# Letting the scheduler place GpSimd's sums on VectorE, and keeping one part's finished weight operands in DRAM for the second token half

## The chip, the cores and the metric

The kernel runs on one core of a Trainium2 chip. The metric is the device time of one execution in microseconds (us). Engines are named as in the profile: PE is TensorE (matmuls; PEld its weight loads), DVE is VectorE, ACT is ScalarE, POOL is GpSimd, SP is SyncE, which here issues nearly all DMAs.

## What is computed

One encoder layer on 2048 tokens of width 1024: windowed grouped-query attention (16 query heads, 4 key/value heads, 64 wide, a window of 128 tokens to either side, a sink logit and a position bias), then a SwiGLU feed-forward net of hidden size 2816. Each sub-layer has an RMSNorm ahead of it and one behind it, and a shift, a scale and a gate made from the conditioning vector `c`.

```python
mod = (c_act @ ada_w[i] + ada_b[i])[:, None, :]
sh1, sc1, g1, sh2, sc2, g2 = jnp.split(mod, 6, axis=-1)
h = rmsnorm(x, mix_norm_pre[i]) * (1.0 + sc1) + sh1
y = windowed_gqa_sink(h, att_w_qkv[j], att_w_o[j], att_sink[j], rel_bias)
x = x + g1 * rmsnorm(y, mix_norm_post[i])
h = rmsnorm(x, ffn_norm_pre[i]) * (1.0 + sc2) + sh2
y = swiglu(h, ffn_w_in[i], ffn_w_out[i])          # (silu(a) * b) @ w_out
x = x + g2 * rmsnorm(y, ffn_norm_post[i])
```

## The kernel before

**Split operands.** Every matmul operand is kept as a high and a low part (fp32r). `split` (l. 788) makes them: ACT casts the high part, DVE (in some places POOL) subtracts it from the source for the low one. `three` (l. 782) then issues three matmuls per product: high by high, high by low, low by high.

**The feed-forward net.** Both projections use a scheme of seven products in place of eight (Strassen's, in Winograd's form) on pairs of tiles. Class `Block` (l. 1359) prepares the weights of one block: two DMAs bring the raw tiles (`wir...`; the profile writes `wiri` for the input projection and `wiro` for the output projection), DVE makes four sums (`s1` to `s4`; `s_i`, `s_o` in the profile), and seven `split`s fill seven `w` tiles (`wa_i`, `ws_i`, `wa_o`, `ws_o`), each one ACT `CAST` and one DVE subtraction. `step(i)` issues the matmuls of product i: 3 per pair of hidden tiles, so 9 for a part of three pairs. `Hidden` (l. 1405) is the input projection. Its results come in pairs of hidden tiles, 11 pairs for each token half, and `give_pair` (l. 1393) writes seven operands of each pair to DRAM (`g_d`); `differences` (l. 1148) makes four of them by sums, two on POOL and two on DVE.

**The output projection.** It runs for token half 0 (1024 tokens) and then for half 1, and each half sums over the 11 pairs in parts: `PARTS = ((2, 3, 3, 3), (3, 3, 3, 2))` pairs. In each part there are four blocks `n2` = 0 to 3 of output columns; the last two are interleaved, and while they run the operands of the next part are loaded (`interleaved`, l. 1448). A part of three pairs has 4 x 7 x 9 = 252 matmuls. The part starts at pair `sum(PARTS[hf][:p])`, so half 1 goes over pairs 0 to 2, 3 to 5, 6 to 8 and at last 9 and 10, which `give_pair` has written without differences, because the last part is done without the scheme (from l. 1657). `Outs.take` (l. 1561) copies the first part's products from PSUM with ACT (`z` tiles, 31 buffers) and adds the later ones on DVE. At the end of a half the seven sums are combined (`COMBINE`, l. 1551; four of the sums on POOL), squared on ACT (`zsq`), summed on DVE (`zacc`), summed over partitions by a matmul with ones, and turned by ACT and DVE into the factor `nrz` (`rstd_out`, l. 1599; one buffer). `finish` (l. 1611) multiplies `z` by `nrz` and adds the residual `zx` on DVE and writes `out`. For half 0 this tail runs beside the first part of half 1.

**What sets the order.** Nothing of this runs in the order of the text. A `Recorder` records every operation with its engine and a cost; `forward` (l. 330) is a list scheduler over the five engines, with a port that DVE and POOL share in its model; `schedule` repeats it and keeps the order that its own model likes best, and `emit` writes that out. So all instructions carry the line of `emit`, L693 (L748 after the change), and are told apart by their tiles. Before the change each operation has one fixed engine. On SP the order is also the scheduler's: a DMA that must wait for a buffer holds those behind it.

**Other places that the prediction names.** In attention, `pr` is a block of probabilities: DVE takes the scores and a maximum (`nm`), ACT the exponential, DVE the reciprocal of the row sum (`rs`), and POOL multiplies (`pr<-pr,rs`, 128x384 or 128x256); then PE transposes it (`ident,pr`), and `phi`, `plo` and `of` are later steps of the same chain. The norm and residual behind attention (`residual`, l. 1135) are `y<-y,no`, `y<-y,xr` and `xacc`; `yacc` is the sum of squares ahead of it; they run beside the last attention blocks and the output projection of attention (`ol`, `wo`).

Of the kernel before, what the change touches and what calls it, by code (L numbers as in the profile page):

```python
# [59 lines left out]
PARTS = ((2, 3, 3, 3), (3, 3, 3, 2))  # L60
MD = max(max(p) for p in PARTS)

# [14 lines left out]
class Op:  # L77
    __slots__ = ("i", "eng", "fn", "args", "kw", "reads", "writes", "occ", "lat", "port", "table", "tiles", "pred", "succ",
                 "start", "end", "put", "prio", "npred", "ready", "ins", "bytes",
                 "wire", "out", "wait", "extra")  # L80
# [53 lines left out]
class Recorder:  # L134
# [41 lines left out]
    def record(self, eng, fn, args, kw):  # L176
# [17 lines left out]
        self.cost(op, [x for j, x in aps if j in out], [x for j, x in aps if j not in out])  # L194
# [20 lines left out]
        return op  # L215

# [113 lines left out]
    def forward(self, ahead, spare):  # L330
# [8 lines left out]
        for o in ops:  # L339
            o.npred, o.ready, o.put, o.wait, o.extra = len(o.pred), 0.0, 0, None, []  # L340
# [3 lines left out]
        port, moved = {"dve": 0.0, "pool": 0.0}, 0  # L344
# [21 lines left out]
        def offer(o):  # L366
            ready = o.ready
            for b in o.tiles:
# [6 lines left out]
            heapq.heappush(soon[o.eng], (ready, o.prio, o.i, o))  # L375

        def drop(heap, o):
            if o in heap[0]:
                heapq.heappop(heap)
            else:  # L380
                heap.pop(next(k for k, x in enumerate(heap) if o in x))
                heapq.heapify(heap)

        def wake(t):
            for u in (t, *t.later):
                if u.parked:
                    again, u.parked = u.parked, []
                    for o in again:
                        offer(o)

# [3 lines left out]
        while n < len(ops):  # L394
            best = None
            for e in ENGINES:
# [3 lines left out]
                while sn and sn[0][0] <= t:  # L400
                    r, p, i, o = heapq.heappop(sn)
                    heapq.heappush(nw, (p, i, o, r))
                if nw:
                    item, begin, src = nw[0], t, nw
                elif sn:
                    item, begin, src = sn[0], sn[0][0], sn
                    item = (item[1], item[2], item[3], item[0])
# [4 lines left out]
                if o.port:  # L412
# [4 lines left out]
            if e == "dve" and o.port and src is now[e] and begin > clock[e] + 150:  # L417
                other = [x for x in now[e] if not x[2].port]
                if other:
                    item = min(other)  # L420
                    o, begin = item[2], clock[e]
                    ask = begin
            if ahead and e in ("act", "dve", "pool") and o.put < 4:
                wait, by = 0.0, None
                for g in (e, *({"dve": ("pool",), "pool": ("dve",)}.get(e, ()) if o.port else ())):
                    for r, p, i, y in soon[g]:
                        if g != e and not y.port:
                            continue
                        if r < begin + o.occ and max(begin - o.prio, begin + o.occ - p) > max(r - p, r + y.occ - o.prio) + 50:
                            w = r + (y.lat + HOP[e] if g != e else 1.0)  # L430
                            if w > wait:
                                wait, by = w, y if g != e else None
                if wait:
                    drop(src, o)
# [3 lines left out]
                    heapq.heappush(soon[e], (wait, o.prio, o.i, o))  # L438
                    continue
            if e == "act" and o.table and o.table != table:  # L440
                stay = [x for x in now[e] if x[2].table in (None, table)]
                near = [x for x in soon[e] if x[3].table == table and x[0] < begin + 900]
                if stay and near:
                    item = min(stay)
                    o, src = item[2], now[e]
                elif near:
                    x = min(near)
                    item, src, o, begin = (x[1], x[2], x[3], x[0]), soon[e], x[3], max(begin, x[0])
            drop(src, o)
# [12 lines left out]
            if y is not None and y.npred < 0 and max(clock[e], o.ready) <= y.start + 20:  # L462
                o.extra = [y]
                begin = max(begin, y.end + HOP[e])
            if e == "act" and o.table and o.table != table:
                table = o.table
# [11 lines left out]
            else:  # L478
                end = begin + o.lat
                if o.port:  # L480
                    port[e] = begin + o.occ
            o.npred = -1
            clock[e] = begin + o.occ + (late if e == "sp" else 0)
# [18 lines left out]
            for q in o.succ:  # L502
                q.npred -= 1
                q.ready = max(q.ready, begin if o.eng == q.eng == "pe" else end + (HOP[q.eng] if o.eng != q.eng else 30))
# [127 lines left out]
    def schedule(self, rounds):  # L632
# [8 lines left out]
        for i in range(rounds):  # L641
# [4 lines left out]
            if best is None or real < best[1]:  # L646
                best = order, real, {b: b.slot for b in self.bufs.values()}, {o: o.extra for o in order if o.extra}
# [3 lines left out]
        self.slots, self.extra = best[2:]  # L651
# [4 lines left out]
    def emit(self, nc, tc, order, outside):  # L656
# [27 lines left out]
        with tc.manual_schedule():  # L684
            for o in order:
                if o.table == "log" and table != "log":
# [21 lines left out]
def encoder_layer(ctx, tc, a):  # L708
# [27 lines left out]
    wo_d = [dram.tile([P, 2, KT, P], F32, name=f"wo_d{n}") for n in range(KT)]  # L736
    cb_d = dram.tile([P, D], F32, name="cb_d")
# [621 lines left out]
    class Block:  # L1359
# [33 lines left out]
    def give_pair(hf, j):  # L1393
# [5 lines left out]
        if hf == S // HALF - 1 and j >= HT // 2 - PARTS[-1][-1]:  # L1399
# [142 lines left out]
    def part_ops(hf, p):  # L1542
        t0 = sum(PARTS[hf][:p])
# [4 lines left out]
    class Outs(Block):  # L1548
# [5 lines left out]
        def __init__(self, ops, hf, part, n2):  # L1554
            t0 = sum(PARTS[hf][:part]) * 2
            ws_ = [a["w_out"][2 * n2 + i, :, t0:t0 + 2 * ops.m] for i in range(2)]
            super().__init__(ops, n2, f"{ops.u}_{n2}", *ws_)
# [99 lines left out]
    t0, m = 2 * sum(PARTS[-1][:-1]), 2 * PARTS[-1][-1]  # L1657
# [105 lines left out]
```

## Time and profile before

| | us |
|---|---|
| runs of the kernel | 3376.76, 2058.2, 2055.8 (median 2058.2) |
| the profiled execution | 2063.44 |
| its span on the core | 2061.7 |
| PE busy | 1998.0 (97%) |
| DVE busy | 1659.1 (80%) |
| ACT busy | 1081.5 (52%) |
| POOL busy | 735.5 (36%) |
| DMA, mean of the span | 192 GB/s |

The page's list of groups says how long one instruction of a kind takes; the table by stretches says how much of a stretch each engine was busy, how much of the clock PE was granted (1.00 is all) and how much the DMAs moved; the list of waits says for which engine and tile PE waited.

The stages by that table: up to 80 us the first norm and the start of the first projection, to about 550 us the rest of it and attention, to 750 us the last attention blocks, the output projection of attention and the norms behind it, to about 1595 us the input projection of the feed-forward net, then the output projection, half 0 to about 1808 us, half 1 to the end.

### The profile page before, as it was taken

The page shows a single profiled execution, that of the slowest core. Times are in us where ns is not written, and L with a number is a line of the kernel's source. Part 1 is how long each engine was busy: PE and PEld are TensorE (multiplying, and loading weights), DVE is VectorE, ACT ScalarE, POOL GpSimd, SP SyncE. Part 2 cuts the span into 40 slices and gives each one's busy share as a digit, 9 for nine tenths or more (in the row PEclk, how much of TensorE's full clock was granted, in tenths as well). Part 3 has the DMA queues.
Part 4 walks back from the last instruction along what each step waited for, and adds up shares of the span by engine and source line. Part 5 has one row for each costly group of instructions (what it writes and reads, how often), then busy time and mean ns, then how long its engine had stood idle before and what let it go on. Part 6 is the DMA issues. An engine that isn't in the chain of part 4 may idle for free.

```text
span 2061.7 us, 28956 instructions
## 1 busy us (share of the span) xinstructions
PE 1998.0 (97%) x9366; PEld 1662.3 (81%) x9366; DVE 1659.1 (80%) x2933; ACT 1081.5 (52%) x2122; POOL 735.5 (36%) x687
## 2 busy tenths in 40 slices
PE   6999999999998999999999999999999999979997
PEld 4888888888787778888888888888888888858886
DVE  7867877765568889887878999776666799989998
ACT  5557766777687864344333633333333744455432
POOL 3413544466978624433435322222221000220030
PEclk9999999999999999999999999999999999999999
DMA  8895765486786695444446843432333554346543
GB/s 296 300 336 198 250 206 197 169 299 214 239 279 215 227 351 170 169 156 171 155 159 228 291 147 136 140 124 91 118 112 112 165 169 164 129 131 242 174 152 108
DMA packets 201667, 396.33 MB, mean 192 GB/s; under 512 B 19195, under 2 KB 61228, under 8 KB 198444
## 3 DMA queue, kind: packets, MB, share of 16 engines
q1 hardware_dynamic: 200940, 393.97, 55.7%
q8 instruction: 74, 1.21, 0.2%
q14 instruction: 77, 0.63, 0.1%
q10 hardware_dynamic: 576, 0.52, 0.1%
HBM read 270.65 MB, written 123.76 MB: 191 GB/s over the span
## 4 chain that ended last, share of the span: by engine, by line
PE 54%; DVE 2%; issue 1%; ACT 1%; POOL 0%; DMA 0%; DVEq 0%; ACTq 0%; POOLq 0%
PE bank L693 54%; DVE z L693 1%; DVE zx L693 1%; ACT nrz L693 0%; POOL z L693 0%; DVE ntz L693 0%; DMA hb22o<-g_d_b 0%; DVE ws_o L693 0%; DVE s_o L693 0%; DVE nrz L693 0%; ACT ws_o L693 0%; ACT zsq L693 0%; POOL p_i L693 0%; DVE zacc L693 0%; ACT L687 0%
## 5 line engine op out<-in xcount | busy, mean ns | idle before, releaser
L693 PE MATMUL bank<-ht,ws_i 128*128 128x512 f32 x1584 | 373.6, 389 | 0.0
L693 PEld LDWEIGHTS bank<-ht,ws_i 128*128 128x128 f32 x1584 | 297.4, 188 | 61.7
L693 PE MATMUL bank<-hb,wa_i 128*128 128x512 f32 x1056 | 254.7, 389 | 0.0
L693 PEld LDWEIGHTS bank<-hb,wa_i 128*128 128x128 f32 x1056 | 198.3, 188 | 41.1
L693 PE MATMUL bank<-ol,wo 128*128 128x512 f32 x768 | 204.0, 397 | 2.2 <-DVE ol L693 1.1
L693 DVE CUSTOM_DVE_ANT_0 pr<-bank,bias,nsink 128x384 f32<-128x384 f32 (+1 forms) x256 | 149.3, 596 | 56.8 <-PE bank L693 55.0
L693 POOL TENSOR_SCALAR pr<-pr,rs 128x384 f32<-128x384 f32 (+1 forms) x256 | 149.7, 603 | 121.6 <-DVE rs L693 115.5
L693 ACT ACTIVATE pr<-pr,nm 128x385 f32<-128x385 f32 (+1 forms) x256 | 154.9, 606 | 71.4 <-DVE nm L693 68.4
L693 POOL TENSOR_TENSOR p_i<-p_i,u_i 128x512 f32<-128x512 f32 x44 | 70.9, 1613 | 311.0 <-ACT wa_i L693 125.9
L693 ACT CAST ws_i<-s_i 128x512 fp32r<-128x512 f32 x132 | 81.9, 620 | 183.1 <-DVE s_i L693 92.9
L693 POOL TENSOR_TENSOR z<-z,z 128x512 f32<-128x512 f32 x32 | 50.2, 1586 | 357.4 <-issue 151.7
L693 DVE TENSOR_TENSOR u_i<-bank,u_i 128x512 f32<-128x512 f32 x176 | 120.7, 688 | 62.5 <-PE bank L693 61.9
L693 PEld LDWEIGHTS bank<-ol,wo 128*128 128x128 f32 x768 | 142.8, 189 | 29.4 <-DVE ol L693 1.5
L693 DVE TENSOR_TENSOR plo<-bank,phi 128x512 fp32r<-128x512 f32 x184 | 120.9, 686 | 30.9 <-ACT phi L693 28.6
L693 PE MATMUL bank<-k,q 128*128 128x384 f32 (+1 forms) x512 | 135.5, 346 | 3.7 <-DVE nm L693 3.7
L693 PE MATMUL bank<-hi,ws 128*128 128x512 f32 x384 | 134.5, 399 | 0.0
L693 DVE TENSOR_TENSOR wa_i<-wiri,wa_i 128x512 fp32r<-128x512 f32 x132 | 114.6, 868 | 21.1 <-ACT wa_i L693 18.4
L693 PE MATMUL bank<-hb,ws_i 128*128 128x512 f32 x528 | 127.0, 389 | 0.6 <-ACT p_i L693 0.6
L693 PE MATMUL bank<-ht,wa_i 128*128 128x512 f32 x528 | 127.0, 389 | 0.0
L693 ACT CAST wa_i<-wiri 128x512 fp32r<-128x512 f32 x132 | 81.1, 620 | 74.3 <-PE bank L693 70.4
L693 DVE TENSOR_TENSOR z<-bank,z 128x512 f32<-128x512 f32 (+1 forms) x164 | 107.6, 661 | 13.3 <-PE bank L693 12.7
L693 PEld LDWEIGHTS bank<-hb,ws_i 128*128 128x128 f32 x528 | 99.1, 188 | 21.5 <-ACT p_i L693 1.0
(245 smaller groups left out, 4526.7 us busy)
## 6 DMA issues: line engine op xcount, KB each, us to landing
wiri<-w_in SPq DMA_DIRECT2D x88, 512.0 KB, 4.7
ada<-ada_w SPq DMA_DIRECT2D x40, 512.0 KB, 5.0
wiro<-w_out SPq DMA_DIRECT2D x48, 384.0 KB, 3.9
q_d<-e SPq DMA_DIRECT2D x32, 512.0 KB, 4.0
q<-q_d SPq DMA_DIRECT2D x16, 1024.0 KB, 6.5
wo<-wo_d SPq DMA_DIRECT2D x16, 1024.0 KB, 5.5
g_d_b<-p_i SPq DMA_DIRECT2D x44, 256.0 KB, 3.4
g_d_t<-p_i SPq DMA_DIRECT2D x40, 256.0 KB, 2.0
```

The source lines that it names most:

```text
L693: o.ins = getattr(engs[o.eng], o.fn)(*args, **kw)
```

## The change

1. **Order of the parts.** A table `FIRST` gives the first pair of each part. Half 0 stays as it was. Half 1 now goes over pairs 2 to 4, 5 to 7, 8 to 10, and at last 0 and 1. `give_pair` follows: pairs 0 and 1 of half 1 are written without differences, 9 and 10 with them.
2. **Kept weights.** Half 0's part 1 and half 1's part 0 are now both over pairs 2 to 4 and so have the same weights. Half 0's part 1 writes each finished `w` tile to DRAM (`wk_d`; 28 writes of 128x768 f32, 384 KB each), and half 1's part 0 loads these (28 DMAs) in place of raw weights, sums and splits. That takes out 8 `wiro` DMAs, 16 DVE sums, 28 ACT `CAST`s and 28 DVE subtractions. SP issues 1220 DMAs in place of 1172.
3. **Placement.** A POOL `tensor_tensor` or `tensor_scalar` may go on DVE. `forward` offers such an operation to both engines and takes the one that is free first; on DVE only if POOL would not end it sooner (`sooner`). DVE has 3077 recorded instructions in place of 2935, POOL 506 in place of 692, ACT 1844 in place of 1872; PE has 9352 in both. So 186 operations move: 79 of the 256 multiplications `pr<-pr,rs` (71 of 128x384, 8 of 128x256), 18 small `pr<-nsink` of 128x4, 71 sums and products of 128x512 (23 of them `u_i<-u_i,b_i`, 11 of the `y` rows, 5 `xacc`, 7 `nacc`, 3 `z`), and 18 subtractions of 128x640 to 128x1024 (`w`, `ol`, `wo`, `ws`).
4. **Turn.** New too: a POOL operation that uses the shared port in the scheduler's model waits for a DVE operation that had itself been held by that port (`turn`).

```diff
+FIRST = ((0, 2, 5, 8), (2, 5, 8, 0))
...
+    def others(self, eng, fn, args, kw, ins):
+
+        if eng == "pool" and fn in ("tensor_tensor", "tensor_scalar"):
+            yield "dve", fn, args, kw
...
+            if len(o.forms) > 1 and e != o.eng_first:
+                t = sooner(o, e, begin)
+                if t is not None:
+                    later(max(begin, t) + 100)
+                    continue
...
+            if e == "pool" and uses and not o.extra and turn is not None and clock[e] - 100 < turn.start < begin:
+                o.extra = [turn]
+                begin = max(begin, turn.end + HOP[e])
+            if e == "dve" and uses:
+                turn = o if begin > ask + 100 else None
...
+    wk_d = [{n: dram.tile([P, 2, PARTS[1][0], P], F32, name=f"wk_d{i}_{n}") for n in ("a11", "s2", "a12", "s3", "s1", "a22", "s4")}
+            for i in range(KT // 2)]
...
-        def __init__(self, ops, i, u, wa, wb):
+        def __init__(self, ops, i, u, wa, wb, keep=None, kept=None):
...
+            if kept:
+                self.w = {}
+                for n, _ in self.STEPS:
+                    self.w[n] = w = pl.tile([P, 2, m, P], F32R, tag="w", bufs=wbufs, name=f"w{n}_{u}")
+                    sp.dma_start(f(w), kept[n])
+                return
...
+                if keep:
+                    sp.dma_start(keep[n], f(w))
...
-        if hf == S // HALF - 1 and j >= HT // 2 - PARTS[-1][-1]:
+        if hf == S // HALF - 1 and 0 <= j - FIRST[-1][-1] < PARTS[-1][-1]:
...
-        t0 = sum(PARTS[hf][:p])
+        t0 = FIRST[hf][p]
...
-            super().__init__(ops, n2, f"{ops.u}_{n2}", *ws_)
+            kept = wk_d[n2] if FIRST[hf][part] == FIRST[1][0] else None
+            super().__init__(ops, n2, f"{ops.u}_{n2}", *ws_, None if hf else kept, kept if hf else None)
...
-    t0, m = 2 * sum(PARTS[-1][:-1]), 2 * PARTS[-1][-1]
+    t0, m = 2 * FIRST[-1][-1], 2 * PARTS[-1][-1]
```

In the rows below a name ends in the program's own numbers: `ws2_o1_0_2` is tile `w` of sum `s2`, output projection, half 1, part 0, block 2.

ACT, where half 1's first part runs and the norm factor of half 0's second 512 tokens (`nrz1_0`) is made. Before:

```order
L693 CAST wa12_o1_0_2_16549<-wiro1_0_2_16356 128x384
L693 COPY z1_1_6_16554<-bank7 128x512
L693 COPY z1_2_0_16566<-bank6 128x512
L693 ACTIVATE nrz1_0_16577<-bank1,epsc_66 128x512
L693 ACTIVATE nrz1_0_16577<-nrz1_0_16577 128x512
L693 ACTIVATE ntz1_0_16586<-nrz1_0_16577 128x512
L693 CAST ws3_o1_0_2_16588<-wiro1_0_2_16356 128x384
L693 CAST ws1_o1_0_2_16591<-s1_o1_0_2_16530 128x384
L693 CAST wa22_o1_0_2_16593<-wiro1_0_2_16356 128x384
L693 CAST ws4_o1_0_2_16596<-s4_o1_0_2_16568 128x384
L693 CAST wa11_o1_0_3_16600<-wiro1_0_3_16495 128x384
L693 CAST ws2_o1_0_3_16615<-s2_o1_0_3_16607 128x384
```

After:

```order
L748 COPY z1_1_6_16550<-bank7 128x512
L748 COPY z1_2_0_16565<-bank3 128x512
L748 COPY z1_3_0_16588<-bank5 128x512
L748 COPY z1_2_1_16608<-bank2 128x512
L748 ACTIVATE nrz1_0_16622<-bank1,epsc_66 128x512
L748 ACTIVATE nrz1_0_16622<-nrz1_0_16622 128x512
L748 ACTIVATE ntz1_0_16634<-nrz1_0_16622 128x512
L748 CAST hb11o1_1_0_16573<-hb11o1_1_0_16573 128x512
L748 COPY z1_3_1_16643<-bank6 128x512
L748 COPY z1_2_2_16650<-bank4 128x512
L748 CAST hb11o1_1_1_16581<-hb11o1_1_1_16581 128x512
L748 CAST wa11_o1_1_0_16663<-wiro1_1_0_16069 128x384
```

Behind the three instructions on `nrz1_0` and `ntz1_0` stood six weight casts of blocks 2 and 3; now operand casts of the next part (`hb11o1_1`) and copies from PSUM stand there, and the first weight cast is the next part's.

SP at the same place (`wk_d2` and `wk_d3` are the kept weights of blocks 2 and 3, `g_d1_5` an operand of pair 5 of half 1). Before:

```order
L693 DMA wiro1_0_2_16356<-w_out 128x768 x2
L693 DMA zx0_0_16435<-x1_d0 128x512
L693 DMA zx0_1_16438<-x1_d0 128x512
L693 DMA zx0_2_16444<-x1_d0 128x512
L693 DMA zx0_3_16457<-x1_d0 128x512
L693 DMA wiro1_0_3_16495<-w_out 128x768 x2
L693 DMA out<-zx0_0_16435 128x512
L693 DMA out<-zx0_1_16438 128x512
L693 DMA zx0_4_16542<-x1_d0 128x512
L693 DMA out<-zx0_2_16444 128x512
L693 DMA zx0_5_16557<-x1_d0 128x512
L693 DMA out<-zx0_3_16457 128x512
```

After:

```order
L748 DMA wa22_o1_0_2_16438<-wk_d2_a22 128x768
L748 DMA ws4_o1_0_2_16460<-wk_d2_s4 128x768
L748 DMA wa11_o1_0_3_16482<-wk_d3_a11 128x768
L748 DMA zx0_0_16490<-x1_d0 128x512
L748 DMA zx0_1_16495<-x1_d0 128x512
L748 DMA zx0_2_16501<-x1_d0 128x512
L748 DMA ws2_o1_0_3_16506<-wk_d3_s2 128x768
L748 DMA zx0_3_16510<-x1_d0 128x512
L748 DMA wa12_o1_0_3_16532<-wk_d3_a12 128x768
L748 DMA ws3_o1_0_3_16548<-wk_d3_s3 128x768
L748 DMA out<-zx0_0_16490 128x512
L748 DMA ws1_o1_0_3_16568<-wk_d3_s1 128x768
```

The raw `wiro` loads of a whole block have become loads of seven finished tiles, which now stand ahead of and between the loads of the residual `zx`, the writes of `out` and the next part's operands.

POOL beside the last attention blocks, where the residual of the second 512 tokens (`y1`) is made. Before:

```order
L693 TENSOR_TENSOR yacc2_6252<-yacc2_6252,ysq2_1_6328 128x512
L693 TENSOR_SCALAR pr13_1_6241<-pr13_1_6241,rs13_1_6266 128x384 x2
L693 TENSOR_TENSOR y1_1_5395<-y1_1_5395,xr1_1_5675 128x512
L693 TENSOR_TENSOR y1_2_5441<-y1_2_5441,no1_6210 128x512
L693 TENSOR_TENSOR y1_3_5641<-y1_3_5641,no1_6210 128x512
L693 TENSOR_TENSOR xacc1_6399<-xacc1_6399,xsq1_1_6415 128x512
L693 TENSOR_TENSOR y1_2_5441<-y1_2_5441,xr1_2_5686 128x512
L693 TENSOR_TENSOR y1_3_5641<-y1_3_5641,xr1_3_6339 128x512
L693 TENSOR_TENSOR xacc1_6399<-xacc1_6399,xsq1_2_6485 128x512
```

After:

```order
L748 TENSOR_TENSOR y1_1_5358<-y1_1_5358,no1_6277 128x512
L748 TENSOR_TENSOR y1_4_5869<-y1_4_5869,no1_6277 128x512
L748 TENSOR_SCALAR pr14_1_6307<-pr14_1_6307,rs14_1_6348 128x384
L748 TENSOR_TENSOR y1_2_5553<-y1_2_5553,no1_6277 128x512
L748 TENSOR_TENSOR y1_3_5674<-y1_3_5674,no1_6277 128x512
L748 TENSOR_SCALAR pr14_1_6307<-pr14_1_6307,rs14_1_6348 128x384 x3
L748 TENSOR_TENSOR y1_6_6040<-y1_6_6040,no1_6277 128x512
L748 TENSOR_TENSOR xacc1_6405<-xacc1_6405,xsq1_1_6476 128x512
L748 TENSOR_SCALAR pr15_1_6378<-pr15_1_6378,rs15_1_6433 128x256 x4
L748 TENSOR_TENSOR y1_3_5674<-y1_3_5674,xr1_3_6398 128x512
L748 TENSOR_SCALAR pr12_2_6462<-pr12_2_6462,rs12_2_6492 128x384
L748 TENSOR_TENSOR y1_4_5869<-y1_4_5869,xr1_4_6478 128x512
```

Seven sums and products of 128x512 stood in a row, from `y1_1<-y1_1,xr1_1` on; now there are at most two in a row, with `pr` multiplications between them, and some, such as `y1_1<-y1_1,xr1_1`, stand on DVE:

```order
L748 TENSOR_TENSOR of12_1_6454<-bank7,low12_1_6427 64x2x128
L748 TENSOR_SCALAR pr12_2_6462<-nsink_125 128x4
L748 TENSOR_TENSOR y1_1_5358<-y1_1_5358,xr1_1_5690 128x512
L748 ISA pr12_2_6462,nm12_2_6473<-bank2,bias2_1111,nsink_125 128x384
L748 ISA nm12_2_6473 128x1
L748 ISA pr15_1_6378,nm15_1_6416<-bank3,bias1_1103,nsink_125 128x256
L748 ISA nm15_1_6416 128x1
L748 TENSOR_TENSOR of12_1_6454<-bank7,low12_1_6427 64x2x128
L748 TENSOR_TENSOR plo13_1_0_6495<-bank4,phi13_1_0_6451 128x512
```

There the moved product stands among the softmax's own instructions (`ISA` is its pass over the scores).

More of the change, by code (lines that the diff above doesn't have):

```diff
@@ L193, in record @@
             op.writes = [(op.writes[0][0], (3, (1 << P) - 1))]
[L194 removed]
+        outs, ins = [x for j, x in aps if j in out], [x for j, x in aps if j not in out]
+        op.forms, op.calls, op.stamp = {}, {}, 0
+        for op.eng, op.fn, op.args, op.kw in (*self.others(eng, fn, args, kw, ins), (eng, fn, args, kw)):
+            self.cost(op, outs, ins)
+            op.forms[op.eng] = op.occ, op.lat, op.port, op.table
+            op.calls[op.eng] = op.fn, op.args, op.kw
+        op.eng_first = eng
         op.pred = {}
@@ L389, in wake, with sooner @@
                         offer(o)
+        def sooner(o, e, begin):
+            end = begin + o.forms[e][1]
+            for f, (occ, lat, _, _) in o.forms.items():
+                if f != e:
+                    t = max(clock[f], o.ready)
+                    for p, i, y, r, k in now[f]:
+                        if p < o.prio and y.npred >= 0 and k == y.stamp:
+                            t += y.forms[f][0]
+                            if t + lat >= end:
+                                break
+                    if t + lat < end:
+                        return t
+            return None
         for o in ops:
@@ L416, in forward @@
             begin, ask, e, o, src, item = best
-            if e == "dve" and o.port and src is now[e] and begin > clock[e] + 150:
-                other = [x for x in now[e] if not x[2].port]
+            if e == "dve" and o.forms[e][2] and src is now[e] and begin > clock[e] + 150:
+                other = [x for x in now[e] if not x[2].forms[e][2] and x[4] == x[2].stamp and x[2].npred >= 0]
                 if other:
```

99 lines of the change are left out of this document (58 added, 41 removed).

## The prediction

> **What bounds the kernel now.** I read the table by stretches first. Its columns are the stretch, its length, then busy time of PE, PEld, DVE, ACT and POOL, the granted clock, the DMA share and GB/s.
>
> ```profile
> 0.00:80.00 80.00, 57.98 (x244) 43.68 (x245) 59.47 (x75) 40.76 (x56) 38.70 (x24) 0.98 0.85 289
> ...
> 250.00:400.00 150.00, 150.00 (x807) 130.18 (x806) 112.74 (x288) 104.01 (x244) 68.27 (x103) 1.00 0.59 198
> 400.00:550.00 150.00, 150.00 (x797) 128.85 (x796) 94.06 (x247) 113.29 (x252) 106.43 (x122) 1.00 0.70 243
> 550.00:640.00 90.00, 79.01 (x396) 65.00 (x395) 62.55 (x142) 65.59 (x145) 67.39 (x78) 0.94 0.69 235
> 640.00:750.00 110.00, 105.27 (x523) 85.77 (x523) 94.18 (x175) 84.56 (x177) 68.00 (x80) 1.00 0.76 267
> 750.00:1180.00 430.00, 429.45 (x1895) 355.28 (x1894) 369.01 (x492) 192.09 (x322) 181.04 (x119) 1.00 0.56 196
> 1180.00:1595.00 415.00, 415.00 (x1832) 343.71 (x1831) 317.32 (x486) 141.25 (x241) 98.37 (x66) 1.00 0.36 124
> 1595.00:1800.00 205.00, 205.00 (x906) 169.80 (x905) 183.77 (x323) 108.02 (x215) 16.86 (x11) 1.00 0.47 156
> 1800.00:1860.00 60.00, 47.60 (x184) 36.22 (x183) 53.75 (x92) 33.75 (x64) 12.67 (x7) 0.89 0.43 134
> 1860.00:2000.00 140.00, 140.00 (x617) 115.81 (x616) 132.29 (x231) 65.39 (x128) 14.58 (x10) 1.00 0.58 198
> 2000.00:2062.00 62.00, 49.08 (x305) 43.98 (x303) 51.73 (x104) 17.34 (x37) 8.98 (x6) 0.92 0.31 106
> ```
>
> PE is busy without a gap in long stretches (415.00 of 415, 205.00 of 205, 140.00 of 140). There only fewer matmuls would help, and the change leaves their number alone. So it can win only where PE lacks time: 22.0 us (80 - 57.98) at the start, 11.0 and 4.7 around the end of attention, 12.4 at 1800 to 1860, 12.9 at the end. To this comes the slower clock: at 1800 to 1860 there are 184 matmuls; at the pace of the stretch ahead (205 / 906 = 0.226 us) they take 41.6 us, so 18.4 us are lost, not 12.4. In 550 to 640 the clock was 0.94 over 90 us, up to 5.4 us, so there 11.0 + 5.4 + 4.7 = 21.1 us are lost up to 750.
>
> Next, for whom PE waits (total, times, longest):
>
> ```profile
> PE bank L693 <- DVE nsq L693: 10.1, 3, 5.7
> PE bank L693 <- DVE of L693: 7.7, 2, 6.4
> PE bank L693 <- ACT hi L693: 7.4, 1, 7.4
> PE bank L693 <- ACT wa_o L693: 7.1, 1, 7.1
> PE bank L693 <- DVE nm L693: 3.7, 3, 2.7
> PE bank L693 <- ACT ws_o L693: 3.4, 2, 2.5
> PE bank L693 <- DVE lo L693: 3.1, 2, 2.4
> PE bank L693 <- DVE wa_o L693: 1.5, 1, 1.5
> PE bank L693 <- POOL w L693: 1.3, 1, 1.3
> ```
>
> `nsq`, `hi`, `lo` and `w` belong to the start, `of` and `nm` to attention. The weight tiles `wa_o` and `ws_o` make 12.0 us, all at the change from half 0 to half 1. Two pieces of the timeline tell how (start, duration, engine, work, and in brackets the idle time before it).
>
> ```profile
> 1850.78 0.69 DVE L693 TENSOR_TENSOR z<-z,nrz 128x512 f32<-128x512 f32 x1
> 1851.56 0.69 ACT L693 ACTIVATE nrz<-bank,epsc 128x512 f32<-128x512 f32 x1 [2.35 <-DVE z L693]
> 1853.48 0.49 ACT L693 CAST ws_o<-wiro 128x384 fp32r<-128x384 f32 x1
> 1855.68 1.22 PE L693 MATMUL bank<-hb11o,wa_o 128*128 128x512 f32 x2 [7.09 <-ACT wa_o L693]
> ...
> 623.62 7.85 DVE L693 TENSOR_TENSOR s_i<-wiri,s_i 128x512 f32<-128x512 f32 x1
> 624.77 2.50 POOL L693 TENSOR_TENSOR y<-y,no 128x512 f32<-128x512 f32 x2
> 628.45 2.47 POOL L693 TENSOR_TENSOR y<-y,xr 128x512 f32<-128x512 f32 x2
> 632.38 0.77 PE L693 MATMUL bank<-phi,v 128*128 128x512 f32 x1 [6.43 <-DVE of L693]
> ```
>
> In the first, ACT stands at the second norm factor, whose one buffer DVE still reads, and the weight casts queue behind it; PE runs dry. In the second, one DVE sum takes 7.85 us while POOL runs its row of sums; the softmax steps queue behind it, and PE waits 6.43 us.
>
> **The change, part by part.** Durations from groups of like instructions (count, busy, mean ns), one timeline row and one DMA row (KB, us to landing):
>
> ```profile
> L693 POOL TENSOR_SCALAR pr<-pr,rs 128x384 f32<-128x384 f32 x224 | 131.2, 604 | 107.5 <-DVE rs L693 103.1 <-DMA wor<-w_o 2.8 <-DVE ntx L693 1.5
> L693 POOL TENSOR_TENSOR u_i<-u_i,b_i 128x512 f32<-128x512 f32 x44 | 65.2, 1483 | 58.8 <-ACT u_i L693 46.1 <-DVE ws_o L693 4.7 <-DVE lh L693 3.8
> L693 POOL TENSOR_TENSOR wo<-wor,wo 128x1024 fp32r<-128x1024 f32 x8 | 19.2, 2404 | 5.4 <-ACT wo L693 5.2
> L693 POOL TENSOR_SCALAR pr<-nsink 128x4 f32<-128x4 f32 x64 | 15.1, 237 | 42.2 <-PE bank L693 40.0 <-DMA k<-k_d 1.1 <-DVE nacc L693 0.9
> L693 DVE TENSOR_TENSOR z<-z,z 128x512 f32<-128x512 f32 x24 | 18.4, 775 | 0.1
> L693 DVE TENSOR_TENSOR wo<-wor,wo 128x1024 fp32r<-128x1024 f32 x8 | 10.9, 1359 | 3.1 <-ACT wo L693 3.1
> L693 DVE TENSOR_TENSOR wa_o<-wiro,wa_o 128x384 fp32r<-128x384 f32 x72 | 43.6, 607 | 1.1 <-ACT wa_o L693 1.0
> L693 ACT CAST wa_o<-wiro 128x384 fp32r<-128x384 f32 x72 | 36.8, 511 | 20.1 <-PE bank L693 18.4 <-DMA wiro<-w_out 1.8
> ...
> 1856.60 0.42 DVE L693 TENSOR_SCALAR ntz<-ntz 128x512 f32<-128x512 f32 x1
> ...
> wiro<-w_out SPq DMA_DIRECT2D x48, 384.0 KB, 3.9
> ```
>
> *Kept weights, reading side.* Out go 28 casts (28 x 0.511 = 14.3 us of ACT) and 44 DVE sums and subtractions (44 x 0.6 = 26 us). What counts is that no weight cast of this part stands behind `nrz` any more, so the 12.0 us of waits and the slow clock behind them lose their cause. Late next is the load of a `w` tile. With 11 buffers and a step of 9 x 0.226 = 2.0 us, a load can be issued some 20 us ahead and lands in about 3.9. The question is the rate, since the loads add 28 x 384 KB = 11.0 MB:
>
> ```profile
> 1810.00:1890.00 80.00, 69.10 (x277) 54.19 (x277) 70.08 (x124) 50.59 (x98) 8.13 (x4) 0.91 0.58 200
> ...
> 1870.00:1880.00 10.00, 10.00 (x46) 8.29 (x45) 7.94 (x14) 6.41 (x13) 0.00 (x0) 1.00 1.04 399
> ```
>
> 1810 to 1890 moved 16.0 MB. Its 277 matmuls need 277 x 0.226 = 62.6 us without stalls. Less three raw blocks (3 x 2 x 384 KB = 2.4 MB) and with 11.0 more it is 24.6 MB, 393 GB/s. The highest rate seen is 399, with PE busy 10.00 of 10. So it just fits, if nothing bunches; some of the operand loads can slip, as their own part begins only later. I take 4 us of new waiting here: a gain of 18.4 - 4 = 14. Bounds: 18.4 (no wait left) and 0 (the loads take the place of the casts).
>
> The Trainium skill, "DMA: Bandwidth & Descriptors", section Specifications, gives about 358 GB/s of HBM per core, which speaks against the change: 24.6 MB would take 68.7 us, 6 more than PE needs, and the gain would be about 12. The trace's 399 GB/s is above that figure, so I go by the trace.
>
> *Kept weights, writing side.* 28 writes, 11.0 MB more while half 0's part 1 takes 252 x 0.226 = 57 us: 193 GB/s on top of the mean of 156. That makes 349, under 399; PE has no gap there. Cost 0, bounds 0 and +4: a `w` buffer is free only when its write has landed (about 3.9 us), of 20 us of buffers.
>
> *Order of the parts.* The sums of pairs 0 and 1 go away and those of 9 and 10 come, at the end of the input projection: eight sums of 0.775 (DVE) to 1.48 us (POOL) and three more writes a pair. PE is busy 415.00 of 415 there, and these pairs are read last but one. 0; bounds 0 and +3. The last part keeps two pairs and its order; the 12.9 us at the end stay.
>
> *Placement.* 79 `pr` multiplications leave POOL (0.604 us each). For DVE no such row exists; the nearest is the one-input 128x512 product of 0.42 us, so at most 79 x 0.42 = 33 us. 71 sums of 128x512 come at 0.775 in place of about 1.48: 55 us on DVE, 105 off POOL. 18 wide ones come at about 1.36 each, 24 us, and 18 of 128x4 at no more than POOL's 0.237, 4 us. DVE gets 33 + 55 + 24 + 4 - 26 = 90 us more, 1749 in all, some 86% of a shorter span. Against one-input products on DVE speaks the Trainium skill, "GPSIMD Engine Reference", section 4.1: only two-input elementwise work is about half as fast on GpSimd, one-input work about equal. By it the 79 would cost 79 x 0.604 = 48 us of DVE; the 0.42 us row, wider than the moved ones, says less.
>
> DVE is not what PE waits for in 250 to 550 (150.00 of 150 twice, DVE 63 to 75% busy). In the input projection, 23 `u_i` products add 23 x 0.775 = 18 us to 369 + 317 of 845. There I cost the added work at 0; the cover is PE's steady queue of ready operands. If it is gone, each moved `pr` holds `nm` up by 0.42 us. The waits for `nm` are 3.7 us now; I add 2.
>
> *The end of attention.* POOL's rows of sums are broken up and `turn` makes POOL let a held DVE operation pass. That takes the 6.43 us wait and part of the slow clock behind it. Of the 21.1 us lost I take half, 10. Bounds: 21 (all), and -9 (DVE at 94 of 110 takes the moved sums of this place, 11 `y` and 5 `xacc`, 16 x 0.775 = 12 us, into 16 idle, and three quarters of it lands on PE).
>
> *Start.* Half of the 128x896 splits `w` go to DVE, which there also makes `lo`. POOL `w` was waited for 1.3 us and DVE `lo` 3.1: bounds 3.1 either way; I take 0.
>
> Sum: -14 - 10 + 2 = -22. The profiled execution took 2063.4 us (span 2061.7) and would take 2041; the median of the runs is 5.2 lower, 2058.2, and gives **2036 us**.
>
> **Rivals.**
> - *The loads bind.* They come in bunches beside `zx`, `out` and the next operands, PE waits for `wk` tiles, and only 4 of 18.4 us are won: 2058.2 - 4 - 10 + 2 = 2046. For it: 393 against 399 GB/s. Against: the loads stand 20 us ahead. The skill's 358, above, lies near this case.
> - *Placement does nothing.* POOL is busy 36% and is the cause of only two of the waits; the port's stalls just move to other instructions. Then only the kept weights count: 2058.2 - 14 + 2 = 2046.
> - *DVE becomes the bound of the softmax: slower.* The 79 moved products stand in DVE's queue among `nm`, `plo` and `of`, which PE needs. If all of them land on PE, it is 2058.2 - 14 + 33 = 2077. It turns into a loss from 34 of 79 on (14 / 0.42). For it: of DVE's time 94 of 110 is taken at 640 to 750. Against: PE has not waited at all at 250 to 550.
> - *More than forecast.* All of 18.4 and 21.1, and 3.1 at the start: 2058.2 - 42.6 = 2016.
>
> **How the numbers follow.** The forecast has 0.42 (2028 to 2042). The two cases at 2046 have 0.17 each, the slower one 0.16, the larger gain 0.08. Low is 2018, near that last case. High is 2062, which leaves out the part of the slower case where more than 43 of the 79 land. A measurement of this kernel tells about 2% (41 us) from no change. Faster by that is below 2017, only the edge of the last case: 0.04. Slower by that, above 2099, needs the slower case and bunching loads together: 0.04. Within: 0.92.
>
> **What would show it.** Right: no wait of PE for `wa_o` or `ws_o` near 1800 to 1860, PE there above 56 of 60 with the clock at 1.00; DMA near 390 GB/s; no DVE sum of 7 us near 623; DVE about 1749 us and POOL about 535 (735.5 - 79 x 0.604 - 71 x 1.48 - 18 x 2.4 - 4). Wrong: waits of PE for DMA of `w_o` tiles (the loads bind); waits for `nm` or `plo` at 250 to 550 (DVE binds); PE in 550 to 750 as before (placement does nothing).

## The result and the profile after

The changed kernel takes **2036.15 us** (median of 4 runs, 2035.73 to 2036.67) against 2057.0 for the kernel before; the two medians stand at 0.990, and the ratio estimated from the single runs is 0.9881 with a 95% interval of 0.9855 to 0.9907. So it is 1.0 to 1.2% faster, clear of noise, though within 2%. The forecast was 2036. That the number is met so closely is partly luck: two of its terms were off in opposite directions and one reason was wrong, as the experiments show.

The table by stretches of the changed kernel, in the columns of the prediction's table:

```profile
0.00:80.00 80.00, 59.28 (x252) 46.11 (x253) 61.75 (x88) 42.50 (x58) 24.29 (x17) 0.96 0.89 305
...
250.00:400.00 150.00, 149.09 (x797) 128.09 (x796) 126.57 (x320) 103.75 (x245) 56.62 (x73) 1.00 0.61 198
400.00:550.00 150.00, 150.00 (x798) 129.56 (x797) 120.14 (x288) 115.35 (x256) 72.67 (x83) 1.00 0.70 243
550.00:640.00 90.00, 86.73 (x448) 71.73 (x448) 79.08 (x193) 70.66 (x164) 54.68 (x63) 0.98 0.78 261
640.00:750.00 110.00, 105.48 (x513) 85.74 (x512) 92.59 (x176) 82.82 (x166) 51.77 (x52) 1.00 0.80 277
750.00:1180.00 430.00, 428.21 (x1888) 353.87 (x1887) 373.83 (x522) 190.14 (x317) 144.00 (x94) 1.00 0.54 192
...
1595.00:1800.00 205.00, 205.00 (x906) 169.76 (x905) 182.81 (x322) 105.87 (x207) 15.03 (x11) 1.00 0.64 222
1800.00:1860.00 60.00, 60.00 (x262) 48.99 (x262) 51.63 (x84) 37.13 (x69) 9.93 (x4) 1.00 0.91 328
```

At 1800 to 1860 PE has no gap and its full clock: 262 matmuls where 184 ran before. At 550 to 640 PE's idle time fell from 11.0 to 3.3 us and the granted clock rose from 0.94 to 0.98; at 640 to 750 it is 4.5 after 4.7. Two small gaps are new: 0.9 us at 250 to 400, and 1.8 at 750 to 1180, where 0.6 was. The list of PE's waits says the same; `wa_o` and `ws_o` are gone from it, and `nm` has fallen from 3.7 to 1.5 us.

```profile
PE bank L748 <- DVE nsq L748: 9.4, 3, 5.8
PE bank L748 <- ACT hi L748: 8.1, 1, 8.1
PE bank L748 <- DVE lo L748: 3.2, 1, 3.2
PE bank L748 <- ACT p_i L748: 1.8, 1, 1.8
PE bank L748 <- DVE nm L748: 1.5, 2, 1.0
...
PE bank L748 <- DVE of L748: 0.7, 1, 0.7
```

While the kept tiles are loaded, the DMA queue moves 400 to 412 GB/s in four windows of 10 us, about the highest rate that the kernel before shows anywhere (403 at 710 to 720), and PE doesn't wait for one of the loads:

```profile
1790.00:1800.00 10.00, 10.00 (x46) 8.28 (x45) 10.00 (x18) 5.16 (x9) 0.00 (x0) 1.00 1.04 408
1800.00:1810.00 10.00, 10.00 (x45) 8.28 (x45) 9.50 (x17) 6.25 (x12) 1.22 (x1) 1.00 1.03 412
1840.00:1850.00 10.00, 10.00 (x46) 8.29 (x45) 9.00 (x16) 7.74 (x16) 0.00 (x0) 1.00 1.05 400
1850.00:1860.00 10.00, 10.00 (x46) 8.29 (x45) 10.00 (x19) 6.33 (x14) 0.00 (x0) 1.00 1.05 401
```

The runs of the kernel before fall into two groups: in one later measurement five of 23 took 2056.3 to 2058.4 us and the other 18 took 2062.2 to 2067.0. The experiments are compared with measurements in which most runs lie in the upper group, so the medians of before there are near 2064, where the first was 2057. What makes the groups is one of the findings.

### The profile page after: what moved, and what is told of

It is laid out like the page before. It is cut to its first block, busy times and chain, and to the rows that moved or that the text cites. A ratio compares the mean times of both kernels' runs of the same rounds, so it can differ in the third digit from the quotient of the medians.

```text
span 2034.9 us, 28945 instructions
## 1 busy us (share of the span) xinstructions
PE 1991.0 (98%) x9366; PEld 1659.3 (82%) x9366; DVE 1703.6 (84%) x3075; ACT 1069.9 (53%) x2094; POOL 554.4 (27%) x501
## 4 chain that ended last, share of the span: by engine, by line
PE 91%; DVE 5%; DMA 2%; issue 1%; ACT 1%; SPq 0%; POOL 0%; DVEq 0%; ACTq 0%; POOLq 0%
PE bank L748 91%; DVE z L748 1%; DVE ada L748 1%; DVE zx L748 1%; DVE pr L748 0%; DMA o_d<-of 0%; DMA ly<-y_d 0%; DMA x<-xT 0%; DMA ol<-o_d 0%; SPq L748 0%; DVE u_i L748 0%; DMA ada<-ada_w 0%; DVE x L748 0%; DVE plo L748 0%; DVE ws_i L748 0%
## 5 line engine op out<-in xcount | busy, mean ns | idle before, releaser
L748 POOL TENSOR_SCALAR pr<-pr,rs 128x384 f32<-128x384 f32 (+1 forms) x177 | 114.7, 660 | 179.7 <-DVE rs L748 168.3
L748 POOL TENSOR_TENSOR z<-z,z 128x512 f32<-128x512 f32 x29 | 45.4, 1577 | 345.9 <-ACT ws_o L748 264.4
L748 DVE TENSOR_TENSOR wa_i<-wiri,wa_i 128x512 fp32r<-128x512 f32 x132 | 103.4, 784 | 19.0 <-ACT wa_i L748 19.0
```

Source lines behind the costliest of these rows:

```text
L748: o.ins = getattr(engs[o.eng], o.fn)(*args, **kw)
```

## The experiments

First come the two halves of the change apart. Where a variant is planned anew, the scheduler finds another order in every stage, so its total differs by a few us for reasons that have nothing to do with the edit; the stage tables count for more.

**Kept weights alone.**

```diff
-        if eng == "pool" and fn in ("tensor_tensor", "tensor_scalar"):
-            yield "dve", fn, args, kw
+        yield from ()
...
-            if e == "dve" and uses:
-                turn = o if begin > ask + 100 else None
```

> The kept weights and the new order of the parts alone; every operation on its fixed engine, no turn. The order is planned anew. Theory (both halves of the change pay, as the two profiles read: 18 us at the change from half 0 to half 1, some 9 us at the end of attention): about 2057 - 18 = 2039 us, 1800 to 1860 without a gap on PE, a loss of PE of some 20 us between 550 and 750 as before. Rival 1 (placement does nothing): 2036 us. Rival 2 (the kept weights give less alone, DVE's relief is needed too): 2046 us, with PE waiting again near 1810 to 1860.

Measured: 2041.45 us, ratio 0.9890 (0.9874 to 0.9907). Its table:

```profile
550.00:640.00 90.00, 85.05 (x436) 71.12 (x435) 59.73 (x152) 70.44 (x156) 73.70 (x87) 0.96 0.74 250
640.00:750.00 110.00, 105.04 (x518) 85.23 (x517) 91.90 (x173) 86.44 (x178) 68.83 (x76) 1.00 0.79 275
1800.00:1860.00 60.00, 60.00 (x261) 48.65 (x260) 49.76 (x82) 37.37 (x68) 13.03 (x6) 1.00 0.91 324
```

The change of halves is as clean as in the full change. But from 550 to 640 us PE is idle 5.0 us and not 11.0, though no operation was moved; a loss "as before" was expected. So most of what I had put down to placement came without it.

**Placement and turn alone.**

```diff
-FIRST = ((0, 2, 5, 8), (2, 5, 8, 0))
+FIRST = ((0, 2, 5, 8), (0, 3, 6, 9))
...
-            kept = wk_d[n2] if FIRST[hf][part] == FIRST[1][0] else None
+            kept = None
```

> Placement and turn alone: raw weights in both halves, the old order of the parts. Planned anew. Theory: the waits for weight casts at the change from half 0 to half 1 stay (PE idle 8 to 12 us there), the end of attention gains some 9 us: about 2048 us. Rival 1 (placement does nothing): 2057 us. Rival 2 (DVE becomes a bound): 2060 us or more, with waits for nm, plo or of between 250 and 550.

Measured: 2052.12 us, ratio 0.9943 (0.9926 to 0.9959). The wait at the change of halves is back at its old length:

```profile
PE bank L748 <- ACT wa_o L748: 7.0, 1, 7.0
PE bank L748 <- DVE zacc L748: 1.8, 1, 1.8
```

Rival 2 falls (no loss on DVE). The gain of 11.5 against 2063.6 is larger than the 9 that theory gave, and, as will be seen, 6 of it is the gap between the two groups.

**The moved operations back on POOL, order kept.**

```diff
-                o.eng = self.at[o]
+                o.eng = o.eng_first
```

> The changed kernel with its order kept as it is, but each of the 186 moved operations issued on POOL again, at its place in the same overall order; the waits of turn stay. Theory (the placement itself pays): POOL gets some 200 us back and DVE loses some 115; the half change stays without a gap, the losses between 550 and 750 grow: 2041 to 2048 us. Rival (only the new order and the turns pay, not the engine): 2035 to 2039 us.

Measured: 2054.08 us, ratio 0.9951 (0.9937 to 0.9966), some 17 us slower than the changed kernel, more than theory said. PE now waits for the softmax's products:

```profile
PE bank L748 <- POOL pr L748: 12.1, 13, 2.6
```

So an order that was made for sharing this work doesn't suit POOL alone. That doesn't make placement a gain of 17 us: the run with fixed engines and an order of its own (2041.45) is only 4 behind.

**Without the waits of turn, order and placement kept.**

```diff
-                o.extra = [turn]
+                o.extra = (turn,)
...
-                for q in self.extra.get(o, ()):
+                for q in self.extra.get(o, ()) if isinstance(self.extra.get(o), list) else ():
```

> The changed kernel with its order and placement kept, but without the waits of turn (a POOL operation no longer waits for a DVE operation that the port had held). Theory (turn is what keeps a DVE sum from standing behind a row of POOL's sums): at least one DVE sum of over 4 us beside the end of attention and PE waiting for it, 2040 to 2043 us. Rival (breaking up the rows of sums is enough): 2034 to 2038 us, no DVE sum of over 3 us.

Measured: 2038.17 us, ratio 0.9875 (0.9859 to 0.9892), against 0.9873 for the changed kernel repeated below: no difference that can be told. A held DVE operation does appear, six us long, behind the end of a row of POOL products and the sum that follows them, but PE still has other work and waits only 0.2 us there:

```profile
691.55 6.31 POOL L748 TENSOR_TENSOR y<-y,nx 128x512 f32<-128x512 f32 x5
694.20 6.00 DVE L748 TENSOR_TENSOR ol<-ol 128x1024 fp32r<-128x1024 f32 x1
```

So `turn` does what it is written for, but the 2040 to 2043 us forecast without it didn't come: by the medians it is worth 1 to 2 us, within the noise.

**Casts ahead of the norm, in the order of before.** My account of the 7.09 us stall was that ACT stood at `nrz` with the casts queued behind it. If so, it is enough to let the casts go first. Only the sequence is edited, where this applies (the body of `casts_first`, some 38 lines, is left out here):

```diff
+        order = self.casts_first(order)
         with tc.manual_schedule():
```

> The kernel before with its order kept, but where squares or norm factors (zsq, nrz, ntz) of half 0 stand right ahead of weight casts of half 1's first part on ACT, these casts go first (what hangs on the norm moves back too). Nothing is left out. Theory (PE waits because the weight casts queue behind a norm that waits for DVE or POOL): the 7.1 us wait falls to 3 or less and the 2.5 us wait behind zsq goes, 6 to 9 us faster than before, without any kept weight. Rival (DVE, busy 53.75 of 60 there, is the limit): the waits move to DVE s_o, ws_o or wa_o, and the time stays within 2 us of before.

Measured: 2063.84 us, ratio 1.0006 (0.9991 to 1.0022). Its runs lie in two groups as well, near 2059 and near 2068, each some 2 to 4 us above those of before (2058 and 2064). No gain, so this theory falls. The timeline of the run says why:

```profile
1857.67 0.55 DVE L732 TENSOR_TENSOR wiro<-wiro 128x384 f32<-128x384 f32 x1
...
1858.26 0.51 ACT L732 CAST ws_o<-wiro 128x384 fp32r<-128x384 f32 x1 [4.59 <-DVE wiro L732]
...
1860.47 1.22 PE L732 MATMUL bank<-hb11o,wa_o 128*128 128x512 f32 x2 [7.43 <-ACT wa_o L732]
```

ACT is free for 4.59 us and waits for a weight sum on DVE, which stands in DVE's queue behind the products `z<-z,nrz` and the residuals `zx`. In the profile of before the same row could have been read:

```profile
1852.70 0.56 DVE L693 TENSOR_TENSOR wiro<-wiro 128x384 f32<-128x384 f32 x1
```

It ends at 1853.26, and the first cast started at 1853.48. The norm factor had held ACT until about then as well; both were late, and taking away one left the other.

**Half 0's residual left out on DVE, alone and with casts first.** The first keeps the order of before; the second moves the casts as in the run above. Both leave half 0's output without its gated part.

```diff
+                if o.eng == "dve" and o.fn == "scalar_tensor_tensor" and o.writes[0][0].name.startswith(("zx0_", "zx1_")):
+                    continue
```

> The kernel before with its order kept; left out are the 16 instructions zx<-z,coef,zx of half 0 on DVE (the gate and the residual; what is written out there is the residual alone). That takes 16 x 0.75 = 12 us of DVE out of the stretch 1830 to 1880 and nothing from ACT. Theory, formed after the casts-first run (DVE's queue is what PE waits for at the change of halves: the weight sums stand in it behind z<-z,nrz and zx): the 7 us wait falls to about 3 or less, since two pairs of zx (4.2 us with what stands between) lie in it; 4 to 7 us faster than before. Rival (ACT's queue, the casts behind nrz): nrz still waits for the last z<-z,nrz, the wait stays at 6 us or more.

> As the run without zx (16 DVE instructions of half 0 left out, what is written there is the residual alone), and the weight casts ahead of the squares and norm factors on ACT as in the casts-first run. Theory (DVE first, ACT's queue only second): at most 2 us better than without zx alone, the wait at the change of halves under 3 us. Rival (both queues count alike): 4 us or more better than without zx alone.

Measured: 2055.73 us, ratio 0.9979 (0.9961 to 0.9997), and with casts first 2062.65, ratio 0.9992 (0.9974 to 1.0011). Both fall into the two groups, so the medians say little; against the same group of before the first is about 2 us faster, the second about 1, where 4 to 7 were expected. The waits tell more. The wait is 4.6 us without `zx` and 4.9 with casts first as well, where 7.1 was. The second run's timeline:

```profile
1842.86 0.55 DVE L734 TENSOR_TENSOR wiro<-wiro 128x384 f32<-128x384 f32 x1
1843.45 0.51 ACT L734 CAST ws_o<-wiro 128x384 fp32r<-128x384 f32 x1 [2.03 <-DVE wiro L734]
...
1845.66 0.89 PE L734 MATMUL bank<-hb11o,wa_o 128*128 128x512 f32 x2 [4.87 <-ACT wa_o L734]
```

DVE's sum is late by itself, and the casts start the moment that it is done. PE then still waits 2.2 us, from 1843.45 to 1845.66, for the fifth cast of the row. Relief of DVE shortens the wait by 2.5 us, which is less than the 4 that I expected; of ACT's queue it is worth nothing on top. In the kept-weights change all three, sums, casts and subtractions, go away. No run takes away the sums alone, so how the 7 us divide among the three stays open.

**One wait in the kernel before.** POOL's sum `y1_1<-y1_1,xr1_1` waits for DVE's `s4_i0_0`, the one of 7.85 us.

```diff
...
+                if o.eng == "dve" and o.writes[0][0].name.startswith("s4_i0_0"):
+                    held, left = o, 1
+                if o.eng == "pool" and held is not None and left and o.writes[0][0].name.startswith("y1_"):
+                    o_extra.append(held)
+                    left -= 1
...
```

> The kernel before with one wait more: at the end of attention POOL's residual sum y1_1<-y1_1,xr1_1 waits for the DVE sum s4 of the first feed-forward block, the one that took 7.85 us. Nothing else changes. Theory (DVE's sum is held while POOL's row of sums runs, and this comes and goes between executions: the runs of before lie near 2057 or near 2063.5, 6 apart, as long as that wait): all runs in the lower group, 6 us under the upper, no DVE sum over 3 us near 623. Rival (the port holds the next DVE sum of the same row instead): no change, another DVE sum of over 4 us near 625.

Measured: 2055.6 us, ratio 0.9967 (0.9956 to 0.9979). All six runs are under 2060, five of them within 2055.2 to 2056.2. In the timeline DVE's sum takes 0.68 us and POOL's row follows:

```profile
624.44 0.68 DVE L693 TENSOR_TENSOR s_i<-wiri,s_i 128x512 f32<-128x512 f32 x1
625.25 1.29 POOL L693 TENSOR_TENSOR y<-y,xr 128x512 f32<-128x512 f32 x1 [0.90 <-POOL pr L693]
```

**Before and after again.**

> The kernel before once more, for a second profile. Theory (two groups of runs, told apart by the held DVE sum near 623): a profile near 2057 has no DVE sum over 3 us there, one near 2063.5 has it. Rival (the groups are chips, or the clock): the sum of about 7.8 us is there in a profile of either time.

> The changed kernel once more, on the same chip as the three others, to set its time and theirs against one and the same kernel before. Theory: 2036 us within 2; if the 6 us of before come and go and those of the changed kernel don't, its runs lie closer together (within 2 us) than those of before.

Measured: before again 2063.74 us, its twelve runs in both groups (2053.62 to 2068.77); after again 2037.21, ratio 0.9873 (0.9859 to 0.9886), its four runs from 2034.72 to 2038.05, more spread than the 2 us expected but not in two groups. Before again was profiled in a run of 2063.91 us and has the held sum. The run without `zx`, which keeps the order of before up to the last stages, was profiled at 2054.06 and hasn't:

```profile
624.31 7.85 DVE L693 TENSOR_TENSOR s_i<-wiri,s_i 128x512 f32<-128x512 f32 x1
```

```profile
624.98 1.72 DVE L695 TENSOR_TENSOR s_i<-wiri,s_i 128x512 f32<-128x512 f32 x1
```

So the same order of instructions runs with and without the 7.85 us, and the groups lie as far apart as that stall is long (PE lost 6.43 us there). Together with the run with one wait, which stays in the lower group, this ties the groups to that one instruction. The casts-first run (profiled at 2067.45, 7.84 us) and the run without `zx` and with casts first (at 2052.50, 1.74 us) fit in. The rivals fall: each of the three later measurements of before has runs in both groups, so they aren't different chips; and two runs without `zx`, 2055.48 and 2062.94 us, have the same granted clock, 0.993. No profile of the kernel before itself in the lower group was taken; that link rests on the runs without `zx`.

**Loads twice.** Meant to find the rate at which the loads bind.

```diff
                     o.ins = getattr(engs[o.eng], o.fn)(*args, **kw)
+                    if o.eng == "sp" and o.reads[0][0].name.startswith("wk_d"):
+                        o.ins = nc.sync.dma_start(*args, **kw)
```

> The changed kernel with its order kept, each of the 28 loads of a kept weight tile issued twice in a row, into the same tile: 11.0 MB more in the stretch where the changed profile already shows 400 to 412 GB/s in four windows of 10 us (338 on the mean of 1780 to 1870). Theory (about 400 GB/s is the most this queue gives, and the loads fit once but not twice): 30.4 + 11.0 = 41.4 MB at 400 GB/s take 103 us, 13 more than the stretch, so 10 to 20 us slower than the changed kernel, with PE waiting for weight tiles between 1800 and 1870. Rival (loads are issued far enough ahead and the rate has room): within 3 us of the changed kernel.

Measured: 2122.0 us, ratio 1.0287 (1.0263 to 1.0312), 85 us slower than the changed kernel. This says nothing on the rate: the second load writes the same tile, so it waits on SP until the first has landed, and all other loads wait behind it.

```profile
1799.74 0.38 SPq L748 DMA_DIRECT2D ws_o<-wk_d_s  x1
1803.92 0.32 SPq L750 DMA_DIRECT2D ws_o<-wk_d_s  x1
...
1805.72 0.42 SPq L748 DMA_DIRECT2D ws_o<-wk_d_s  x1
1811.04 0.32 SPq L750 DMA_DIRECT2D ws_o<-wk_d_s  x1
```

The 28 pairs hold the queue for 3.5 to 5.4 us each, 119 us together, which is more than the 85 that were lost. How near 412 GB/s is to a limit stays open.

**Only sums on DVE**, the `pr` products all on POOL.

```diff
-        if eng == "pool" and fn in ("tensor_tensor", "tensor_scalar"):
+        if eng == "pool" and fn == "tensor_tensor":
```

> The changed kernel, but only two-operand sums and products may go to DVE; the 256 multiplications pr<-pr,rs stay on POOL. Planned anew. In the changed profile the moved ones took 0.62 us on DVE on the mean (0.42 in the middle), 0.60 on POOL before. Theory (they gain nothing on DVE): 2034 to 2038 us, as the changed kernel. Rival (they take POOL off the softmax's path): 2040 us or more, with waits of PE for POOL pr between 540 and 680, as when all were put back on POOL.

Measured: 2040.93 us, ratio 0.9896 (0.9876 to 0.9915). By the time the rival is nearer, but the run doesn't decide. PE waits 2.8 us in five pieces for `POOL pr` between 500 and 760 (1.2 in the changed kernel), while the largest loss there, 3.0 us, is one wait for ACT `ol`. And this order is behind from the start: by 250 us PE has done 1111 matmuls where the changed kernel has done 1131, some 4.5 us at 0.226 each, with waits for `hi`, `nsq`, `w` and `lo` and none for the softmax's products. So only a part of the 4 us can be the moved products.

## Why the prediction was right, and where not

**Kept weights, the size.** I took 14 of 18.4 us, with 4 left for late loads. That term was mis-sized: nothing was left, PE at 60.00 of 60. The 393 GB/s of my working didn't come either. The loads were spread over 55 us, nine of the 28 before 1800, and the mean was 328 from 1800 to 1860 and 338 from 1780 to 1870; only four windows of 10 us reached 400 to 412, without a wait of PE. And 399 was not the highest rate of the kernel before, as I wrote:

```profile
710.00:720.00 10.00, 10.00 (x46) 8.27 (x45) 9.93 (x10) 9.34 (x16) 5.68 (x3) 1.00 1.05 403
```

The Trainium skill's figure that I weighed ("DMA: Bandwidth & Descriptors", section Specifications, about 358 GB/s of HBM per core) lies below these windows, and the traces disagree with it there. On the mean the loads stayed under it, so what a longer stretch above it would cost isn't shown.

**Kept weights, the reason.** The step that failed is "What counts is that no weight cast of this part stands behind `nrz` any more". Casts in front of `nrz` gained nothing: PE's wait for `wa_o` was 7.4 us where 7.1 was. The weight sums in DVE's queue were as late as the casts, and behind them the casts take 2.2 us more. The 26 us of DVE work that the change removes, which I named and then set aside, belong to the cause; their share alone was not measured.

**The end of attention.** I took 10 us, half of what is lost there, for placement and turn. PE's idle time and clock there did improve by about as much (idle 15.7 to 7.8, clock 0.94 to 0.98). But the kernel before without the held sum, the run with one wait, stands at

```profile
550.00:640.00 90.00, 85.45 (x441) 70.97 (x440) 60.91 (x160) 72.33 (x164) 75.19 (x89) 0.98 0.78 259
640.00:750.00 110.00, 105.14 (x515) 85.41 (x514) 96.52 (x169) 85.30 (x173) 62.47 (x71) 1.00 0.77 273
```

against 86.73 and 105.48 for the full change: 1.6 us are left for placement there (0.6 by the repeated profile, 85.55 and 105.62). So the step of my sum that put 10 us here down to placement and turn was wrong: nearly all of the gain is one stall, which a new order avoids without them as well.

**The base.** I set -22 against the median, 2058.2. The runs in the lower group hardly have the held sum, so 6 of my 10 us were not there to be won from that median, and the 4.4 us too few at the change of halves made up for most of it: -22 + 6 - 4.4 = -20.4, where 2057.0 to 2036.15 is -20.9. The cleaner comparison is: 2055.6 (before, held sum avoided) to 2037.2 (changed, same measurement) is 18.4 us, about what was lost at the change of halves (18.4 in the first profile; in that of the run with one wait 189 matmuls in those 60 us, so 17.3 by the same working). Against the upper group, near 2064, the held sum comes on top. That the 5.2 us between the profiled execution and the median pointed at a stall that comes and goes, I didn't ask.

**Placement on DVE.** 79 `pr` products were to cost at most 33 us at 0.42 each. The row of the change:

```profile
L748 DVE TENSOR_SCALAR pr<-pr,rs 128x384 f32<-128x384 f32 x71 | 42.9, 618 | 1.3
```

With the eight of 128x256 they took some 48 us, so "at most 33" was wrong. The mean of the 71 is 0.618 us, the median over all 79 is 0.42, and single ones took up to 2.36. 31 of the 79 took more than 0.5 us, and each of these began while a POOL instruction was running, so the mean holds waits for POOL. The Trainium skill's section 4.1 of "GPSIMD Engine Reference" (one-input work about equal on both) comes out right for the mean, beside POOL's 0.604, not for the median. DVE was to have 1749 us and has 1703.6, in part since its other sums are held less (`s_i<-wiri,s_i` 745 ns on the mean after 1068; without the held sum, in the run with one wait, 880); POOL has 554.4 where I said 535. The 2 us that I added for new waits came, not at `nm` but as the gaps at 250 to 400 and 750 to 1180. The kept weights alone have neither gap, placement and turn alone have both. The first shows the slower rival (DVE binds the softmax) at work once: a moved product takes 2.29 us beside a wide subtraction on POOL, and PE waits for the `plo` behind it:

```profile
275.61 2.40 POOL L748 TENSOR_TENSOR ws<-wsr,ws 128x1024 fp32r<-128x1024 f32 x1
275.94 2.29 DVE L748 TENSOR_SCALAR pr<-pr,rs 128x384 f32<-128x384 f32 x1
278.89 0.50 PE L748 MATMUL bank<-plo,v 128*128 128x512 f32 x1 [0.91 <-DVE plo L748]
```

As a whole that rival didn't happen. "Placement does nothing" was nearly right in its mechanism. The start, which I took as 0, brought about as much as the new gaps cost: by 250 us PE has done 1131 matmuls (1141 in the repeated profile) where 1121 were done before, some 2 us or more at 0.226 each. The writes and the order of the parts (0) are as forecast: PE is at 205.00 of 205 from 1595 to 1800 in the changed kernel too.

## What to carry to other kernels

When PE waits for engine A and A waits for engine B, look at when each of A's other inputs was ready too: a wait names only the last to come, and taking it away may leave one that was 0.2 us earlier. A profiled execution that lies 5 us above the median may hold a stall that the median doesn't have; set each term of the sum against the execution that has it. Before a planner's new freedom is given the credit, let the old freedom plan anew: here a new order alone avoided the same stall.

## What the runs showed of the hardware

A DVE sum with two operands in SBUF that starts 0.1 us after a POOL sum can be held not for that one alone but for the whole row: in three profiles (2063.44, 2063.91 and 2067.45 us) it took 7.84 or 7.85 us and ended behind six POOL sums of some 1.25 us that follow each other without a gap, where it takes 0.68 alone. In two others (2054.06 and 2052.50 us), with the same row, it got in behind the first sum, took 1.72 or 1.74 us, and POOL's next two took 2.99 us in the first of these, where two had taken 2.50:

```profile
624.88 1.27 POOL L695 TENSOR_TENSOR y<-y,xr 128x512 f32<-128x512 f32 x1
624.98 1.72 DVE L695 TENSOR_TENSOR s_i<-wiri,s_i 128x512 f32<-128x512 f32 x1
626.11 2.99 POOL L695 TENSOR_TENSOR y<-y,no 128x512 f32<-128x512 f32 x2
```

The Trainium skill ("SBUF — State Buffer", section "SBUF: two separate sides") says that the one that starts first has the shared pair for its instruction and the other waits. The two short cases agree; the three long ones show that the one that waits need not be the next to go. What decides is not shown: in all five the DVE sum starts 0.10 to 0.12 us after the first POOL sum.
